# A recurrence beside a projection: plain operand layout, and its steps placed by hand in TensorE's order

## Chip, cores, metric

One NeuronCore of a Trainium2 chip runs the whole program. The metric is the device time of one execution in microseconds (us), as the median of several runs. A profiled execution of the same program is read for the reasons.

## What is computed

One encoder block over 2048 tokens of width 1024. A normed input goes through one projection with 3328 output columns. The first 1792 feed an RWKV-7 mixer with 8 heads of 64, the rest a differential attention with 4 heads. Both results go through an output projection, and a gated convolutional feed-forward layer follows. The change is about the mixer, whose core is this recurrence over the tokens:

```python
def step(S, inp):
    r_t, w_t, k_t, v_t, a_t, b_t = inp
    sa = jnp.einsum('bhvk,bhk->bhv', S, a_t)
    S = (S * w_t[:, :, None, :] + sa[..., None] * b_t[:, :, None, :]
         + v_t[..., None] * k_t[:, :, None, :])
    return S, jnp.einsum('bhvk,bhk->bhv', S, r_t)
```

The mixer around it shifts the projected columns by one token, makes decay, rate and gate from them, normalizes each head's output, adds a bonus term and multiplies by the gate. Everything is held in float32. The large products split each operand into a high and a low part and add three products.

## The kernel before

**Stages.** `phase1` projects four token blocks of 512 tokens. For the mixer's 14 column groups of 128 (`proj_rwkv`, then `shift`) it takes 24 matmuls of 512 columns each, for token blocks 0 to 3. Then come the attention's columns in six groups of 256 (`proj_qk`, `proj_v` by way of `token_major`), 96 matmuls of 256 columns each, for token blocks 3, 0, 1, 2, so 24 groups in all. While token blocks 1 and 2 go through, nine pieces of attention (`head`) are started. After that, attention and feed-forward follow until the end (L968 is a line of the latter).

**The recurrence.** `rwkv(u)` handles a unit of 128 tokens, as two chunks of 64, for all 8 heads (4 pairs `i` times 2 halves `hd`); there are 16 units. A unit loads its columns from DRAM and makes head norms (`st`, then a reciprocal root on VectorE in some dozen small operations, then `nx`, transposed as `nb`), decay (`lpw`) and rate (`lpa`), and products with cumulated decays (`xm`, `bk`). TensorE forms the score products `sa`, and VectorE masks them. A 64-row triangular system has to be inverted per head and chunk. Its 32-row diagonal parts go through DRAM (`ed`) into `el`, are eliminated on VectorE by 31 pairs of dependent operations (`tl`, `wl`, L482 and L483) and return by `wd` into `tt`; `zp` adds the remaining corner. Then the two chunks run one after the other: `gp`, `up`, `hu` and the output `y`, with ScalarE or VectorE between them; the state goes from chunk to chunk. The tail normalizes and gates `y` and writes `yd`.

**Layout.** `xm` and `sh` hold per head a 128-row operand in which one half belongs to the state and the other to the chunk's tokens, and which half is which depends on the chunk and the head. So `gp` is one product of 128 rows, while `y` is a sum of two products for each head, which are issued in turn:

```python
for hd in range(2):
    for i in range(GP):
        nc.tensor.matmul(y4[yq, i, hd, :], xm[c][:, i, hd, C:2 * C], sh[c][:, i, hd, :], start=True, stop=False)
        nc.tensor.matmul(y4[yq, i, hd, :], rb[ub, i, hd, :], su[c][ub, i, hd, :], start=False, stop=True)
```

**Order.** The order of the instructions on every engine is fixed when the program is built, by a scheduler that takes ready work by priority. `unit()` starts one unit behind each two column groups and lets a unit that was started two units earlier go on; both with a priority raised by `HP = 3000`. So the recurrence's products stand wherever the scheduler's own clock saw them ready, in the middle of the projection's.

Of the kernel before, what the change touches and what calls it, by code (L numbers as in the profile page):

```python
# [28 lines left out]
XUB = 7  # L29
SUB, LRB, PUB, UB = 3, 3, 3, 2  # L30
# [9 lines left out]
LAG = 2  # L40
HP, HA1, HA = 3000, 400, 0
# [98 lines left out]
def phase1(g, ctx):  # L140
# [38 lines left out]

    def spread(tb):  # L180

        rs = rsa[:, 4 * tb:4 * tb + 4]
        rx = dn.tile([P, 4, P], F32, name="rx", tag="x", bufs=XB)
        nc.vector.tensor_copy(rx, rs.unsqueeze(2).broadcast_to((P, 4, P)))
        ps = ps_mm.tile([P, 4, P], F32, name="tp", tag="mm")
# [19 lines left out]
    def proj_rwkv(tb, hT, b, w=None, ps=None):  # L205
# [26 lines left out]
    def token_major(tb, hT, gi):  # L232
# [4 lines left out]
        for jj in range(2):  # L237
            for q in range(KT // 2):
                for j2 in range(2):
# [6 lines left out]
                    if q == KT // 2 - 1:  # L246
                        yield 2 * jj + j2, ps

    def proj_qk(tb, hT, gi):
# [12 lines left out]
        return lambda: finish_qk(tb, gi, qz, rs)  # L262

    def finish_qk(tb, gi, qz, rs):
# [3 lines left out]
        for hl_ in range(2):  # L268
# [15 lines left out]

    def proj_v(tb, hT, gi):
# [5 lines left out]

    w = load_w("w_in_a", 12, 4, P, True)
# [3 lines left out]
    stats(0)  # L296
    rb = spread(0)
# [9 lines left out]
    mask = cp.tile([P, P], F32, name="mask")  # L307
    nc.sync.dma_start(out=mask, in_=a["c_mask"])
# [42 lines left out]
    for i in range(UB):  # L351
        tts.append(cp.tile([P, NCH, GP, C], F32, name=f"tt{i}"))
# [5 lines left out]
    hc = cp.tile([P, GP, C], F32, name="hc")  # L358
    nc.vector.memset(hc, 0.0)
    def rwkv(u):  # L360
# [8 lines left out]
        r = sp.tile([P, GP, SB], F32, name="zl", tag="zl", bufs=1)  # L369
# [3 lines left out]
        xm = [sp.tile([P, GP, 2, P], F32, name="xm", tag="xm", bufs=XUB) for c in range(NCH)]  # L373
        bk = [sp.tile([P, GP, P], F32, name="bk", tag="bk", bufs=XUB) for c in range(NCH)]
        rb = sp.tile([P, GP, 2, C], F32, name="rb", tag="rb", bufs=(XUB + 1) // 2)
        lr = sp.tile([P, NCH, GP, C], F32, name="lr", tag="lr", bufs=LRB)
# [8 lines left out]
        nst = 2 * GP  # L385
        nrm = sp.tile([P, nst], F32, name="nrm", tag="nrm")
        rsqrt(g, sp, nrm, st.rearrange("p i h -> p (i h)"), 1.0, L2_EPS, nst, "k")
        nx = sp.tile([P, nst, 64], F32, name="nx", tag="tmp", bufs=2)
        nc.scalar.copy(nx, nrm.unsqueeze(2).broadcast_to((P, nst, 64)))

        lpw = ps_tp.tile([P, GP, SB], F32, name="lpw", tag="tp")
# [9 lines left out]
        for p in range(GP):  # L401
            nc.scalar.activation(kh[:, p], lpa[:, p], AF.Tanh, bias=hw0[:, 4 + p:5 + p], scale=0.5)
        nb = ps_tp.tile([P, GP, SB], F32, name="nb", tag="tp")
# [17 lines left out]
        for c in range(NCH):  # L421
            cs, kc, uc = slice(c * C, c * C + C), slice(c * C, c * C + C), slice(C - c * C, 2 * C - c * C)
            for hd in range(2):
                q = hb[hd]
                nc.vector.tensor_mul(xm[c][q, :, hd, 0:C], kkn[q, :, cs], pp[q, :, c, 0:C])
                if hd == 0:
                    nc.vector.tensor_mul(bk[c][:, :, uc], kkn[:, :, cs], an[:, :, cs])
                nc.vector.tensor_mul(xm[c][q, :, hd, C:2 * C], r[q, :, cs], pp[q, :, c, 1:C + 1])
            nc.vector.tensor_mul(bk[c][:, :, kc], kh[:, :, cs], pin[:, :, cs])
# [4 lines left out]
        nc.gpsimd.tensor_mul(rkh, kh, r)  # L434
        sb = ps_tp.tile([P, GP, 2], F32, name="sb", tag="tp")
# [5 lines left out]
        def mk(q, a, b):  # L441
            return mask[q, a:b].unsqueeze(1).broadcast_to((64, GP, b - a))

        for c in range(NCH):
            for hd, q, q_ in ((0, lo_, hi_), (1, hi_, lo_)):
                sa = ps_sc.tile([P, GP, P], F32, name="sa", tag="sa")
                for i in range(GP):
                    nc.tensor.matmul(sa[:, i, :], bk[c][q, i, :], xm[c][q, i, hd, :], start=True, stop=True)
                kb, ub = hb[c], hb[1 - c]
# [4 lines left out]
        bkt = bk  # L454
        for c in range(NCH):
            ps = ps_sc.tile([P, GP, P], F32, name="bt", tag="sa")
            bs = bk[c]
            for i in range(GP):
                nc.scalar.activation(bs[:, i], bs[:, i], AF.Identity, scale=pc[:, i, c])
                nc.tensor.transpose(ps[:, i, :], bs[:, i, :], ident)  # L460
            nc.scalar.copy(bkt[c], ps)
# [3 lines left out]
        cp3 = lambda t: t.rearrange("s c p t -> s (c p) t")  # L465
        for hd in range(2):
            for hf in range(2):
                r = slice(hd * 64 + hf * 32, hd * 64 + hf * 32 + 32)
                nc.sync.dma_start(out=ed[hd, hf].rearrange("g s t -> s g t"), in_=cp3(lr[r, :, :, hf * 32:hf * 32 + 32]))
# [16 lines left out]
        yield  # L486
        for hd in range(2):
            for hf in range(2):
                r = slice(hd * 64 + hf * 32, hd * 64 + hf * 32 + 32)
                nc.sync.dma_start(out=cp3(tt[r, :, :, hf * 32:hf * 32 + 32]), in_=wd[hd, hf].rearrange("g s t -> s g t"))  # L490
        t11 = sp.tile([P, NCH, GP, 32], F32, name="t11", tag="t11")
        for hd in range(2):
            r1 = slice(hd * 64, hd * 64 + 32)
            nc.vector.transpose(t11[r1].rearrange("s c p t -> s (c p) t"), tt[r1, :, :, 0:32].rearrange("s c p t -> s (c p) t"))
# [4 lines left out]
        nc.sync.dma_start(out=zg, in_=g.zd[tb, 13, :, sl])  # L499
        su = [sp.tile([P, GP, 2, C], F32, name="su", tag="su", bufs=SUB) for c in range(NCH)]  # L500
        sh = [sp.tile([P, GP, 2, C], F32, name="sh", tag="sh", bufs=SUB) for c in range(NCH)]
# [6 lines left out]
        for c in range(NCH):  # L508
            for hd in range(2):
                nc.scalar.copy(sh[c][hb[1 - hd], :, hd], v4[hb[c], :, hd])  # L510
            nc.scalar.copy(su[c][hb[c]], v4[hb[c]])

        zt = sp.tile([P, NCH, GP, 32], F32, name="zt", tag="gt")
# [624 lines left out]
```

## Time and profile before

| | |
|---|---|
| median of 3 runs | 3273.06 us (3269.57 to 3291.25) |
| profiled execution, its own time | 3270.93 us |
| its span, first to last instruction | 3269.2 us |
| TensorE busy | 3136.8 us (96%) |
| VectorE busy | 2085.0 us (64%) |
| ScalarE busy | 1524.9 us (47%) |
| mean granted TensorE clock | 0.972 |

In the profile PE is TensorE (PEld its weight loads), DVE VectorE, ACT ScalarE, POOL GpSimd, SP the queue that issues the DMAs. L569 is line 569 of the kernel. Float32 products appear as two records each, so 16 records stand for 8 products; transposes and the products of the projections have one. A record's duration is not the time that TensorE gives to it, because matmuls overlap; that is read from one start to the next.

### The profile page before, as it was taken

Reading aid. Unit: us, or ns where it says so; the run is one execution under the profiler, and the core shown is the slowest. Engines: PE = TensorE matmul, PEld = TensorE weight load, DVE = VectorE, ACT = ScalarE, POOL = GpSimd, SP = SyncE. Lnnn points to the kernel's source line nnn. Section 1 sums busy time; section 2 is a strip of 40 time slices with the busy share of each in tenths; the row PEclk is TensorE's granted clock in tenths of the full one; section 3 lists DMA queues with packets and bytes.
Section 4 is the critical chain, followed back from the end, with each engine's and each line's share of the span. In section 5 each row is a group of like instructions: output and inputs, shape, how many; then the busy total and the mean of one; then the engine's idle time right before and its main releaser. Section 6 shows DMA issues by size and latency. Waiting matters only on the chain.

```text
span 3269.2 us, 54217 instructions
## 1 busy us (share of the span) xinstructions
PE 3136.8 (96%) x19314; PEld 2657.6 (81%) x19314; DVE 2085.0 (64%) x5939; ACT 1524.9 (47%) x3391; POOL 661.0 (20%) x501
## 2 busy tenths in 40 slices
PE   8999999999999898899999999999998999999999
PEld 6777777888888788788878888888888888888887
DVE  4788778888873565667777786666533444444444
ACT  5666555655645564444445565444423322222221
POOL 4112113342322013254444111111100000000000
PEclk9989999989999899999999999999999999999999
DMA  9765544345464977556556756565574132223222
GB/s 298 252 210 155 189 141 152 105 134 153 126 183 132 290 233 262 160 192 204 197 196 222 234 174 203 168 206 184 192 281 153 65 116 84 97 91 107 87 97 97
DMA packets 395006, 557.43 MB, mean 171 GB/s; under 512 B 82544, under 2 KB 209776, under 8 KB 394608
## 3 DMA queue, kind: packets, MB, share of 16 engines
q1 hardware_dynamic: 394736, 553.97, 52.9%
q8 instruction: 153, 2.51, 0.3%
q14 instruction: 117, 0.96, 0.1%
HBM read 440.59 MB, written 113.25 MB: 169 GB/s over the span
## 4 chain that ended last, share of the span: by engine, by line
PE 80%; DMA 9%; DVE 8%; ACT 1%; issue 1%; SPq 1%; POOL 0%; DVEq 0%; ACTq 0%; POOLq 0%
PE up L968 9%; PE up L966 9%; PE up L967 9%; PE dn L1010 5%; PE dn L1009 5%; PE dn L1011 5%; PE mm L213 3%; PE mm L211 3%; PE mm L212 3%; PE mm L243 2%; PE y L571 2%; PE y L569 2%; PE mm L244 2%; PE mm L245 2%; PE up L906 2%; DMA fwlo<-lo_w_out 2%
## 5 line engine op out<-in xcount | busy, mean ns | idle before, releaser
L967 PE MATMUL up<-hT,fwhi 128*128 128x512 f32 (+1 forms) x1536 | 581.3, 379 | 0.0
L966 PE MATMUL up<-hT,fwhi 128*128 128x512 f32 (+1 forms) x1536 | 575.4, 378 | 3.7 <-DVE halo L975 2.8
L968 PE MATMUL up<-hT,fwlo 128*128 128x512 f32 (+1 forms) x1536 | 571.6, 378 | 7.0 <-DMA fwlo<-lo_w_ffn_up 7.0
L973 DVE SCALAR_TENSOR_TENSOR yy<-up,vec,yy 128x511 f32<-128x511 f32 x352 | 262.0, 744 | 346.2 <-ACT yy L970 345.9
L1012 DVE TENSOR_TENSOR acc<-dn,acc 128x512 f32<-128x512 f32 x352 | 237.0, 688 | 184.0 <-PE dn L1011 183.2
L968 PEld LDWEIGHTS up<-hT,fwlo 128*128 128x128 f32 x1536 | 292.2, 190 | 62.6 <-DMA fwlo<-lo_w_ffn_up 10.4
L966 PEld LDWEIGHTS up<-hT,fwhi 128*128 128x128 f32 x1536 | 290.2, 190 | 57.8 <-issue 4.3
L967 PEld LDWEIGHTS up<-hT,fwhi 128*128 128x128 f32 x1536 | 291.9, 190 | 52.4
L996 POOL TENSOR_TENSOR gl<-yy,gh 128x512 fp32r<-128x512 f32 (+1 forms) x64 | 106.0, 1656 | 1006.4 <-ACT gh L995 821.8
L117 ACT CAST fwhi<-fwraw 128x1024 fp32r<-128x1024 f32 x164 | 172.5, 1052 | 266.1 <-PE up L967 185.5
L970 ACT ACTIVATE yy<-up,vec 128x512 f32<-128x512 f32 x176 | 136.6, 777 | 301.2 <-PE up L968 295.9
L1010 PE MATMUL dn<-dlo,gh 128*128 128x512 f32 x704 | 276.1, 393 | 0.9 <-DMA dlo<-lo_w_ffn_down 0.9
L729 DVE CUSTOM_DVE_ANT_0 e<-sc,nd 128x512 f32<-128x512 f32 (+3 forms) x320 | 188.3, 607 | 136.9 <-PE sc L726 112.9
L1009 PE MATMUL dn<-dhi,gh 128*128 128x512 f32 x704 | 272.5, 396 | 0.5 <-ACT gh L995 0.5
L1011 PE MATMUL dn<-dhi,gl 128*128 128x512 f32 x704 | 261.9, 393 | 0.1
L243 PE MATMUL mm<-whi,hh 128*128 128x256 f32 x768 | 232.7, 304 | 11.9 <-DVE qlo L105 5.4
L244 PE MATMUL mm<-wlo,hh 128*128 128x256 f32 x768 | 227.2, 297 | 7.7 <-DMA wlo<-lo_w_in_b 7.5
L245 PE MATMUL mm<-whi,hl 128*128 128x256 f32 x768 | 225.0, 296 | 0.0
L736 ACT ACTIVATE e<-e,nm 128x1024 f32<-128x1024 f32 (+4 forms) x192 | 171.9, 898 | 53.3 <-DVE nm L733 52.9
L211 PE MATMUL mm<-hh,whi 128*128 128x512 f32 x448 | 187.8, 421 | 9.2 <-ACT hh L201 6.9
L117 ACT CAST whi<-wraw 128x512 fp32r<-128x512 f32 x208 | 127.8, 619 | 138.5 <-PE mm L212 61.8
L213 PE MATMUL mm<-hh,wlo 128*128 128x512 f32 x448 | 187.2, 419 | 2.1 <-POOL wlo L119 2.1
(278 smaller groups left out, 7322.6 us busy)
## 6 DMA issues: line engine op xcount, KB each, us to landing
fwraw<-in_w_ffn_up_dram SPq DMA_DIRECT2D x132, 512.0 KB, 5.5
fwlo<-lo_w_ffn_up SPq DMA_DIRECT2D x88, 512.0 KB, 5.0
draw<-in_w_ffn_down_dram SPq DMA_DIRECT2D x132, 256.0 KB, 4.3
vg<-vd SPq DMA_DIRECT2D x128, 256.0 KB, 4.3
wraw<-in_w_in_a_dram SPq DMA_DIRECT2D x112, 256.0 KB, 3.5
wraw<-in_w_in_b_dram SPq DMA_DIRECT2D x96, 256.0 KB, 5.1
lo_w_ffn_up<-fwlo SPq DMA_DIRECT2D x44, 512.0 KB, 2.9
dlo<-lo_w_ffn_down SPq DMA_DIRECT2D x88, 256.0 KB, 4.9
```

What stands on the lines that cost most here:

```text
L117: nc.scalar.copy(hi, raw)
L211: nc.tensor.matmul(ps, whi[k], hh[k], start=k == 0, stop=False)
L213: nc.tensor.matmul(ps, wlo[k], hh[k], start=False, stop=k == KT - 1)
L243: nc.tensor.matmul(ps, hh[k][:, ts_], whi[k], start=k == 0, stop=False)
L244: nc.tensor.matmul(ps, hh[k][:, ts_], wlo[k], start=False, stop=False)
L245: nc.tensor.matmul(ps, hl[k][:, ts_], whi[k], start=False, stop=k == KT - 1)
L966: nc.tensor.matmul(ps[:, q], wh[:, k % 4, cs], xh, start=k == 0, stop=False)
L967: nc.tensor.matmul(ps[:, q], wh[:, k % 4, cs], xl, start=False, stop=False)
L968: nc.tensor.matmul(ps[:, q], wl[:, k % 4, cs], xh, start=False, stop=k == KT - 1)
L1009: nc.tensor.matmul(ps, gh_[:, tsl], dh_, start=gi == 0, stop=False)
L1010: nc.tensor.matmul(ps, gh_[:, tsl], dl_, start=False, stop=False)
L1011: nc.tensor.matmul(ps, gl_[:, tsl], dh_, start=False, stop=gi == FG - 1)
```

## The change

It rewrites the recurrence's layout and the place of its steps.

- **Layout.** `ar` and `bk` hold per pair and chunk 128 plain rows (both heads), made by four products on VectorE where there were twelve; the masked scores of a chunk and head become one tile `sm`, by one masking where there were three. The state is kept block by block in `hs`. In the chunk loop one product of 128 columns per pair (`ar` by `h`) gives what `gp` and the first half of `y` gave; two further groups of 8 products (with `sm`) add the tokens' parts. The copies into `sh`, and the operand `rb`, are gone.
- **Steps.** `rwkv` yields between its steps: ten up to the inverse, four from its result to `zp`, six for the two chunks, four for the tail. `tick()` runs after every 6 matmuls of a mixer projection and after every 12 of an attention projection, and issues the next steps of up to three units. Inside `manual_schedule` TensorE takes its instructions in the order of the source. The other engines' order is still the scheduler's, now without the raised priority (`HP = 0`). It closes when the last unit has finished.
- **Moved.** `spread` (row norms) goes behind the first projection of a token block, the transposes of `finish_qk` into the next group's pieces, the reciprocal root of the head norms behind `lpa`.

```diff
+XUB, SMB = 3, 6
+UNITS = 3
+HP, HA1, HA = 0, 400, 0
@@ proj_rwkv, in the loop over k
             nc.tensor.matmul(ps, wlo[k], hh[k], start=False, stop=k == KT - 1)
+            if k % 2:
+                tick()
@@ token_major, in the loop over q
+                tick()
+                if 4 * jj + q in (4, 6) and fins:
+                    fins.pop(0)()
@@
+    order = ExitStack()
+    order.enter_context(tc.manual_schedule(engines={mybir.EngineType.PE}))
+    def step(n, to):
+        with tc.high_priority(offset=HP):
+            if stage[n] and next(stage[n][0], "next") == "next":
+                unit = stage[n].pop(0)
+                if to:
+                    stage[to].append(unit)
+    def tick():
+        nonlocal ticks
+        ticks += 1
+        st = stage
+        if not st["chain"] and st["ready"]:
+            st["chain"].append(st["ready"].pop(0))
+        behind = len(st["ahead"]) + len(st["inverse"]) + len(st["ready"])
+        if not st["inverse"] and not st["ready"] and (len(st["ahead"]) > 1 or st["ahead"] and not st["first"] and (not units or behind + len(st["chain"]) == UNITS)):
+            st["inverse"].append(st["ahead"].pop(0))
+        behind = len(st["ahead"]) + len(st["inverse"]) + len(st["ready"]) + len(st["chain"])
+        if not st["first"] and units and (units[0] + 1) * SB <= done * TB and behind < UNITS:
+            st["first"].append(rwkv(units.pop(0)))
+        if ticks % 2:
+            step("chain", "last")
+            if ticks % 8 == 1 or not st["chain"]:
+                step("first", "ahead")
+        else:
+            step("last", None)
+            step("inverse", "ready")
+            step("first", "ahead")
@@ rwkv
+        yield
         lpa = ps_tp.tile([P, GP, SB], F32, name="lpa", tag="tp")
...
+        yield
+        nst = 2 * GP
+        nrm = sp.tile([P, nst], F32, name="nrm", tag="nrm")
+        rsqrt(g, sp, nrm, st.rearrange("p i h -> p (i h)"), 1.0, L2_EPS, nst, "k")
...
+        nc.vector.tensor_mul(ar4[:, :, 1:3], ch(kkn), pp[:, :, :, 0:C])
+        nc.vector.tensor_mul(bk4[:, :, 1:3], ch(kkn), ch(an))
+        nc.vector.tensor_mul(ar4[:, :, 0::3], ch(r), pp[:, :, :, 1:C + 1])
+        nc.vector.tensor_mul(bk4[:, :, 0::3], ch(kh), ch(pin))
...
-                nc.vector.tensor_mul(lr[q, c], sa[ub, :, 0:C], mk(ub, 0, C))
-                nc.vector.tensor_mul(rb[ub, :, hd], sa[ub, :, C:], mk(ub, C, P))
-                nc.vector.tensor_mul(xm[c][q_, :, hd], sa[kb], mk(kb, 0, P))
+                    nc.tensor.matmul(sa[:, i, :], bk[q, i, c], ar[q, i, c], start=True, stop=True)
+                nc.vector.tensor_mul(sm[c][:, :, hd], sa, mk[c])
+            yield
...
+        for c in range(NCH):
+            kb, ub, h, h_ = hb[c], hb[1 - c], hs[c], hs[1 - c]
+            hp = sp.tile([P, GP, C], F32, name="hp", tag="hp")
+            for hd, q in enumerate(hb):
+                nc.gpsimd.tensor_mul(hp[q], h[q, :, hd], pc[q, :, c].broadcast_to((64, GP, C)))
+            gy = ps_y.tile([P, GP, 2, C], F32, name="gy", tag="y")
+            for i in range(GP):
+                nc.tensor.matmul(gy[:, i], ar[:, i, c], h[:, i], start=i == 0, stop=False)
+            for n, (i, hd) in enumerate(ih):
+                nc.tensor.matmul(gy[ub, i, hd], sm[c][kb, i, hd, ub], su[c][kb, i, hd], start=False, stop=n == len(ih) - 1)
+            gt = sp.tile([P, GP, 2, C], F32, name="gt", tag="gt")
+            nc.scalar.copy(gt[ub], gy[ub])
+            yield
+            up = ps_ch.tile([P, GP, 2, C], F32, name="up", tag="ch")
+            for i, hd in ih:
+                nc.tensor.matmul(up[ub, i, hd], tt[ub, i, hd], gt[ub, i, hd], start=True, stop=True)
+            nc.scalar.copy(su[c][ub], up[ub])
+            yield
+            hu = ps_ch.tile([P, GP, C], F32, name="hu", tag="ch")
+            for hd, q in enumerate(hb):
                 for i in range(GP):
+                    nc.tensor.matmul(hu[q, i], bk[:, i, c, q], su[c][:, i, hd], start=True, stop=True)
+            for hd, q in enumerate(hb):
+                nc.vector.tensor_add(h_[q, :, hd], hu[q], hp[q])
+            for n, (i, hd) in enumerate(ih):
+                nc.tensor.matmul(gy[kb, i, hd], sm[c][:, i, hd, kb], su[c][:, i, hd], start=False, stop=n == len(ih) - 1)
+            nc.scalar.copy(yt[kb], gy[kb].rearrange("p i h d -> p (i h d)"))
+            yield "next" if c == NCH - 1 else None
```

## Rows read from the trace of the kernel before

**Rows 1.** Page part 4, chain that ended last, by engine.
```profile
PE 80%; DMA 9%; DVE 8%; ACT 1%; issue 1%; SPq 1%; POOL 0%; DVEq 0%; ACTq 0%; POOLq 0%
```

**Rows 2.** By stretch: length, busy us (instructions) of PE, PEld, DVE, ACT, POOL; clock; DMA share, GB/s.
```profile
100.00:572.00 472.00, 466.89 (x3204) 371.21 (x3204) 387.01 (x1270) 279.97 (x702) 93.42 (x93) 0.93 0.58 179
572.00:1050.00 478.00, 455.41 (x4264) 400.96 (x4263) 364.74 (x1195) 276.51 (x895) 145.80 (x134) 0.94 0.47 139
1050.00:1230.00 180.00, 157.12 (x1124) 145.92 (x1124) 106.29 (x487) 110.97 (x373) 23.44 (x17) 0.92 0.82 252
```

**Rows 3.** Timeline of TensorE, 579 to 606 us: start, us, engine, line.
```profile
580.62 0.97 PE L559 MATMUL hu<-su,bk 128*64 128x64 f32 x16
581.51 0.38 PE L243 MATMUL mm<-whi,hh 128*128 128x256 f32 x1
...
582.06 0.33 PE L569 MATMUL y<-sh,xm 128*64 128x64 f32 x2
582.32 0.32 PE L571 MATMUL y<-su,rb 64*64 64x64 f32 x2
582.58 0.33 PE L569 MATMUL y<-sh,xm 128*64 128x64 f32 x2
...
590.10 1.16 PE L399 MATMUL lpa<-zw,wda 64*128 64x128 f32 x8
591.19 0.38 PE L245 MATMUL mm<-whi,hl 128*128 128x256 f32 x1
```

**Rows 4.** Table by stretch, around two falls of the granted clock.
```profile
579.00:585.80 6.80, 6.80 (x64) 5.52 (x62) 5.62 (x19) 4.88 (x26) 1.53 (x2) 1.00 0.10 39
585.80:589.20 3.40, 3.40 (x27) 3.07 (x27) 3.02 (x11) 1.50 (x4) 0.11 (x1) 0.50 0.12 36
...
633.00:637.00 4.00, 0.00 (x0) 0.00 (x0) 3.73 (x11) 0.00 (x0) 1.49 (x2) 1.00 0.15 58
637.00:640.40 3.40, 3.32 (x15) 3.10 (x15) 3.32 (x9) 1.87 (x5) 1.54 (x2) 0.50 0.55 161
```

**Rows 5.** Groups by line, VectorE, 100 to 1050 us: busy us, mean ns | idle before.
```profile
L452 DVE TENSOR_TENSOR xm<-sa,mask 64x512 f32<-64x512 f32 x64 | 44.1, 689 | 1.0
L428 DVE TENSOR_TENSOR xm<-zl,pp 64x256 f32<-64x256 f32 x64 | 30.3, 473 | 4.1 <-PE y L569 3.9
L425 DVE TENSOR_TENSOR xm<-kkn,pp 64x256 f32<-64x256 f32 x64 | 29.6, 463 | 19.5 <-PE y L569 18.6
L450 DVE TENSOR_TENSOR lr<-sa,mask 64x256 f32<-64x256 f32 x64 | 27.0, 422 | 27.1 <-PE sa L448 25.8
L451 DVE TENSOR_TENSOR rb<-sa,mask 64x256 f32<-64x256 f32 x64 | 26.7, 418 | 0.8
L420 DVE TENSOR_TENSOR an<-an,pin 128x512 f32<-128x512 f32 x16 | 12.4, 778 | 3.9 <-ACT pin L414 2.5 <-ACT an L416 1.4
```

**Rows 6.** DMA issues, 100 to 1050 us: KB each, median us to landing.
```profile
el<-ed SPq DMA_DIRECT2D x128, 64.0 KB, 2.2
...
ed<-lr SPq DMA_DIRECT2D x64, 32.0 KB, 1.6
wd<-wl SPq DMA_DIRECT2D x64, 32.0 KB, 2.0
tt<-wd SPq DMA_DIRECT2D x64, 32.0 KB, 1.9
```

**Rows 7.** Timeline of VectorE: the inverses' first operation; longest; last.
```profile
134.04 0.19 DVE L482 TENSOR_TENSOR tl<-wl,el 128x31 f32<-128x31 f32 x1 [0.36 <-DMA el<-ed]
...
779.33 0.18 DVE L482 TENSOR_TENSOR tl<-wl,el 128x31 f32<-128x31 f32 x1
...
835.16 0.16 DVE L483 TENSOR_TENSOR wl<-wl,tl 128x8 f32<-128x8 f32 x1
...
934.48 1.05 DVE L482 TENSOR_TENSOR tl<-wl,el 128x31 f32<-128x31 f32 x1
...
966.69 0.17 DVE L483 TENSOR_TENSOR wl<-wl,tl 128x8 f32<-128x8 f32 x1
```

More of the change, by code (lines that the diff above doesn't have):

```diff
@@ L267, in finish_qk, with piece @@
         nc.gpsimd.tensor_mul(q3, q3, rs.unsqueeze(2).broadcast_to((P, 16, 64)))
-        for hl_ in range(2):
+        def piece(hl_):
             h = (gi - 7) % 2 * 2 + hl_
@@ L290, in proj_v @@
             nc.sync.dma_start(out=g.vd[t0:t0 + P, :, (gi - 11) * 256:(gi - 10) * 256], in_=vs.bitcast(F32))
+    units = list(range(g.ntb * TB // SB))
+    stage = {n: [] for n in ("first", "ahead", "inverse", "ready", "chain", "last")}
+    done = ticks = 0
+    order = ExitStack()
[26 more added lines that the diff above has]
+            step("first", "ahead")
     w = load_w("w_in_a", 12, 4, P, True)
@@ L522, in rwkv @@
-        for hd in range(2):
-            r1 = slice(hd * 64, hd * 64 + 32)
-            r2 = slice(hd * 64 + 32, hd * 64 + 64)
-            for c in range(NCH):
-                for i in range(GP):
-                    nc.tensor.matmul(zp[r1, 1, c, i, :], zt[r2, c, i, :], tt[r2, c, i, 32:64], start=True, stop=True)
-            nc.scalar.copy(tt[r1, :, :, 32:64], zp[r1, 1])
-        for hd in range(2):
-            q = slice(hd * 64, hd * 64 + 64)
-            nc.vector.tensor_copy(sh[0][q, :, hd, :], hc[q])
@@ L574, in rwkv @@
-        nh, w = 2 * GP, GP * P
+        yield
+        zt = sp.tile([P, GP, 2, 32], F32, name="zt", tag="gt")
+        zp = ps_sc.tile([P, 2, GP, 2, 32], F32, name="zp", tag="sa")
+        ih = [(i, hd) for i in range(GP) for hd in range(2)]
+        for b in range(2):
+            r1 = slice(b * 64, b * 64 + 32)
+            r2 = slice(b * 64 + 32, b * 64 + 64)
+            for i, hd in ih:
+                nc.tensor.matmul(zp[r2, 0, i, hd], sm[1 - b][r1, i, hd, r2], t11[r1, i, hd], start=True, stop=True)
@@ new lines, in rwkv @@
+        for b in range(2):
+            r2 = slice(b * 64 + 32, b * 64 + 64)
+            nc.scalar.copy(zt[r2], zp[r2, 0])
+        yield
+        for b in range(2):
+            r1 = slice(b * 64, b * 64 + 32)
+            r2 = slice(b * 64 + 32, b * 64 + 64)
+            for i, hd in ih:
+                nc.tensor.matmul(zp[r1, 1, i, hd], zt[r2, i, hd], tt[r2, i, hd, 32:64], start=True, stop=True)
+        for b in range(2):
+            r1 = slice(b * 64, b * 64 + 32)
+            nc.scalar.copy(tt[r1, :, :, 32:64], zp[r1, 1])
@@ L593, in rwkv @@
         nc.gpsimd.tensor_add(yt, yt, vt)
+        yield
+        yield
+        yield
+        y = ps_sc.tile([P, w], F32, name="y", tag="sa")
+        nc.tensor.matmul(y, zg, wgu, start=True, stop=True)
         nc.vector.tensor_mul(yt, y, yt)
         nc.sync.dma_start(out=g.yd[u * SB:(u + 1) * SB, :], in_=yt)
-    units = list(range(g.ntb * TB // SB))
-    started = []
-    def unit():
-        if units:
-            with tc.high_priority(offset=HP):
-                started.append(rwkv(units.pop(0)))
-                next(started[-1])
-        if started and (len(started) > LAG or not units):
-            with tc.high_priority(offset=HP):
-                next(started.pop(0), None)
     def head():
@@ L611, in head, with after @@
             next(g.heads, None)
-    def after(done):
-        if (units and (units[0] + 1) * SB <= done * TB) or (started and not units):
-            unit()
-        if not units and not started and g.att is None and 2 in g.phases:
+    def after():
+        if not units and not any(stage.values()) and g.att is None and 2 in g.phases:
+            order.close()
             rctx.close()
@@ L630, in phase1 @@
                     continue
-                shift(tb, b, proj_rwkv(tb, hT, b), rb)
+                ps = proj_rwkv(tb, hT, b)
+                rb = rb or spread(rx)
+                shift(tb, b, ps, rb)
             if gi == 0 and tb + 1 < nb:
-                stats(tb + 1)
-            after(tb)
+                rx = stats(tb + 1)
+        done = tb + 1
     nh = 0
@@ L648, in phase1 @@
                 nh += 1
-    while units or started:
-        after(nb)
+    while units or any(stage.values()):
+        tick()
+    after()
     if 2 not in g.phases:
```

177 lines of the change are left out of this document (59 added, 118 removed).

## The prediction

> **What bounds the kernel now.** The first view is the chain of work that ended last: four fifths of it is TensorE [rows 1]. So I look for the stretch in which the change lies and ask what TensorE does there. The table by stretch gives it: from 100 to 572 us the mixer's projections of token blocks 1 to 3 run with the recurrence between them, from 572 to 1050 the attention's projections with the rest of the recurrence, and by 1230 the projections are over [rows 2]. In the 950 us of the first two, TensorE idles only (472.0 - 466.9) + (478.0 - 455.4) = 27.7 us. VectorE is busy 387 + 365 = 752 us of them, 79%: much, but not the bound. Work on VectorE, ScalarE or the queues is therefore worth only what it makes TensorE wait; TensorE's own time is worth all of it. Yet its busy time hides two losses. The first is in its timeline, read from start to start: 16 records of `hu` take 581.51 - 580.62 = 0.89 us, 0.056 each, while the records of `y`, no wider, take 582.58 - 582.06 = 0.52 us for four, 0.13 each [rows 3]. These alternate between two shapes, 128*64 and 64*64; those of `hu` do not. The second is the granted clock, 0.93 and 0.94 in the two stretches [rows 2]. It has two levels, so it stood at the lower, 1.2 GHz, for 2 x 0.07 x 472 + 2 x 0.06 x 478 = 123 us. If all of that were matmul time, half of it, 62 us, is lost.
>
> **The sum is made against the profiled execution**, 3270.93 us, whose span is 3269.2; it lies 2 us under the median of the runs. After 1230 us nothing is edited, and the chain that ended last is mostly TensorE's work [rows 1], so a gain before it should arrive at the end nearly whole.
>
> **Layout on TensorE.** Per chunk, `gp` (16 records at 0.056, 0.9 us) and `y` (32 records at 0.13, 4.1 us) are 5.0 us. They become 4 products of 128 columns and two groups of 8 small ones, each group of one shape. The 128-column records are priced by `lpa`, 8 records in 591.19 - 590.10 = 1.09 us; each group of 16 records by `hu`, 0.89 us [rows 3]. That is 2.9 us, so 2.1 us less for each of 32 chunks: **-68 us**. `up`, `hu`, `sa` and `zp` keep count and shape. This is the surest term, because TensorE is the bound where it lies. Its low end, if one of the two small groups cost per record what those of `lpa` do (0.136), is 1.3 us less per chunk, -27; for more than 68 there is no row.
>
> **Clock.** At 585.8 the clock fell although TensorE had been busy for all of the 6.8 us before, most of it `y` in turns; at 637 it fell after 4 us of idleness [rows 4]. Both causes exist. The first kind should mostly go, since the alternation is gone and no more than two or three short steps stand between two pieces of projection; the second follows the waits. I take half of the 62 us: **-30**, with ends 0 and -62. The Trainium skill (TensorE: Matmul & The Clock Gate, Part 1, "What's actually happening") makes idleness what returns the clock to its lower level. By that rule alone the change would return nothing here, and the sum would be 30 us higher; the fall at 585.8, behind a fully busy stretch, speaks against taking the rule alone.
>
> **Waits of TensorE in order.** Before, the scheduler put a product where it saw it ready and filled the time with projection. Now a step whose operand is late stops everything behind it: the next piece of projection, and through it the evictions of `shift` and `finish_qk` and the next units' steps. Counting ticks in the diff, the steps run over 280 ticks, from the first projection of token block 1 to the 14th of the 24 attention groups, so a tick lasts some 881 / 280 = 3.1 us. The chunk steps stand two ticks apart, 6 us for one copy or addition: covered. `nb` stands three or four ticks behind `st`, `sa` two or three behind `nb`; with VectorE three quarters busy these are tight. `lpw` and `lpa` follow `st` one tick apart in one PSUM buffer, which VectorE or ScalarE must have read first. `zp` waits for the inverse and is the subject of a rival. No row shows these waits. One end is that all goes well and the old idleness vanishes too, -28; the other is the rival's. I take **+25**, about as much again as the 27.7 us that the scheduler's own fixed order left [rows 2], since it too is an order that cannot be changed when something is late.
>
> **Other engines.** Masking takes 4 x (422 + 418 + 689) = 6.1 us per unit and becomes four operations priced like the longest, 2.8 us; `xm` takes 4 x (473 + 463) = 3.7 us and becomes two of 128 x 512 at 778 ns, 1.6 us [rows 5]. So VectorE loses 5.5 us per unit, 88 us in all, the `bk` products, the state copies and ScalarE's copies into `sh` apart. That is counted at nothing, because TensorE's work covers it; if VectorE were the bound it would be worth up to 88. It shortens the waits above. The unit's DMAs (three loads, `ed`, `el`, `wd`, `tt`, two loads, one store) stay the same in number on SP's queue but lose their raised priority, and `hp` on POOL is of the same size; both are hidden by several ticks. Hand-overs between projection and recurrence cost a little at each place; there were as many before, so nothing. `spread` behind the first projection removes a short wait per token block, included in the old idleness.
>
> **Tail.** The last unit ends in the 14th attention group instead of the 16th, and the pieces of attention start one group later. From 1050 to 1230, without recurrence to fill in, TensorE idles 22.9 us over a third of the groups, DMA being busy 0.82 of the time [rows 2]. That is almost 3 us per group, so **+4** for one and a half more groups; ends 0 and 15.
>
> Sum: -68 - 30 + 25 + 4 = -69, so **3202 us**.
>
> **Rivals.**
>
> *B, everything falls into place.* No waits and a full clock: -68 - 62 - 28 + 4 = -154, 3117 us. For it: the steps are spaced with some slack, and VectorE has less to do. Against it: the tight places named above.
>
> *C, slower: the inverse comes later than its step.* The step that stores `ed` and the first `zp` stand 17 ticks apart for every second unit and 26 for the others, 53 and 81 us. The way between takes 1.6 + 2.2 + 2.0 + 1.9 = 7.7 us of DMA [rows 6] and the inverse, 62 operations in a row on VectorE: 56.0 us for the longest, 32.4 for the last, when VectorE has little else [rows 7]. In the middle (44) it needs 52 us and is just covered; at 56 it needs 64, and TensorE stands still for 11 us in eight units, 88 us, and loses some 14 more to the clock behind each idleness [rows 4]. That is -69 + 88 + 14 = +33, 3304 us. It is slower than before from an inverse of about 52 us on. For it: the raised priority is gone. Against it: VectorE's share falls from 79% to (752 - 88) / 881 = 75%, and while TensorE stands still little new work reaches VectorE. The Trainium skill (SBUF — State Buffer, "Who interferes with whom") lets GpSimd and a VectorE operation with both inputs in SBUF lock each other out; by that rule the inverse stays long whatever TensorE does, as its operations are of this kind and GpSimd's work does not shrink. That is this rival, at its price.
>
> *D, no change: the inverses set the pace.* `el` and `tl` have one buffer, so inverses run one after another; from the first operation at 134.0 to the last at 966.9 there are 833 us for 16, 52 us per unit [rows 7]. If that pace is VectorE's own and not TensorE's, the stretch keeps its length and what TensorE saves turns into waiting: 3265 to 3275 us. Against it: that is some four times 62 operations at the 0.16 to 0.19 us that the first and last of them show, so most of an inverse's time is other work pushed between.
>
> **Chances and range.** The forecast 0.53, B 0.16, D 0.14, C 0.17. A difference under 1%, 33 us, is about what cannot be told from no change here. Under 3238 us lie B and nearly all of the forecast: faster 0.66. D, and the edges of the forecast and of C, are the same: 0.19. Slower 0.15. The range goes from B's 3117, with a little for the layout's far end, to C: 3110 to 3300.
>
> **What would show it.** After: the records of the two new groups with `sm` stand about 0.06 us apart, and `gy` on the whole takes some 3 us per chunk; the granted clock between 100 and 1000 us is 0.96 or more; TensorE's idleness there is between 40 and 70 us, spread over `nb`, `sa` and `zp`; the last `yd` is issued near 970 us; the stretch after the projections keeps its length. The prediction is wrong if waits of `zp` for VectorE's or the DMA's `tt` stand out (C), if the inverses lie end to end while TensorE idles (D), or if the clock stays at 0.93 though nothing waits.

## The result and the profile after

The changed kernel takes 3310.34 us (median of 4 runs, 3303.41 to 3322.34) against 3277.88 for the kernel before (4 runs). The ratio is 1.0111, 95% interval 1.0077 to 1.0145: slower by 1.1%, where 3202 us was forecast. Its profiled execution has a span of 3301.6 us, 32.4 more than before. The chain of work that ended last still is mostly TensorE's, but less so than in [rows 1], and DMA and VectorE have more of it:

```profile
PE 69%; DMA 13%; DVE 10%; ACT 3%; issue 2%; SPq 2%; POOL 1%; DVEq 0%; ACTq 0%; POOLq 0%
```

The table by stretch, with the columns and the bounds of [rows 2]:

```profile
100.00:572.00 472.00, 432.71 (x3165) 347.04 (x3166) 336.77 (x1134) 269.77 (x649) 100.83 (x100) 0.91 0.54 163
572.00:1050.00 478.00, 425.43 (x3939) 385.26 (x3938) 321.33 (x1071) 267.45 (x819) 143.77 (x129) 0.92 0.51 148
1050.00:1230.00 180.00, 147.62 (x1068) 138.51 (x1068) 98.07 (x436) 111.59 (x404) 19.98 (x14) 0.91 0.77 239
```

Read the first two numbers of a row (its length, and what TensorE is busy of it) against each other: TensorE idles 39.3 + 52.6 = 91.9 us in the first two stretches, where it idled 27.7 before. The clock is 0.91 and 0.92 instead of 0.93 and 0.94, although VectorE has 94 us less to do. What TensorE waits for there (instruction, what it waited for: us in total, times, longest):

```profile
PE lpw L440 <- DVE rq_x_k L87: 15.6, 4, 10.9
PE sb L491 <- POOL rkh L486: 13.3, 5, 5.3
PE nb L459 <- ACT kh L450: 8.0, 7, 2.4
```

`zp`, the step of rival C, is not among the first twelve of that list. The longest wait shows how such a thing comes about. The timeline of the kernel after (start, us, engine, line; in brackets the idle time before and what ended it):

```profile
890.92 1.64 SPq L517 DMA_DIRECT2D ed<-sm  x2
...
896.30 0.18 DVE L87 TENSOR_SCALAR rq_x_q<-qss 128x16 f32<-128x16 f32 x1 [2.63 <-ACT qsq L264]
898.82 0.80 SPq L523 DMA_DIRECT2D el<-ed  x2
899.00 0.28 PE L247 MATMUL mm<-whi,hl 128*128 128x256 f32 x1
901.27 3.57 SPq L523 DMA_DIRECT2D el<-ed  x5
908.90 0.19 DVE L530 TENSOR_TENSOR tl<-wl,el 128x31 f32<-128x31 f32 x1 [12.43 <-DMA el<-ed]
909.93 0.16 DVE L87 TENSOR_SCALAR rq_x_k<-st 128x8 f32<-128x8 f32 x1
910.15 2.07 PE L440 MATMUL lpw<-zw,wda 64*128 64x128 f32 x8 [10.87 <-DVE rq_x_k L87]
```

`lpw` is written to the one PSUM buffer that `st` was written to (PSUM is where this kernel puts its products). It comes free when the first operation of the reciprocal root has read `st` (`rq_x_k`). That operation is ready, but it stands in VectorE's queue behind the first operation of the other unit's inverse (`tl`), and this waits 12.43 us for `el`. So a late transfer stops VectorE, and through it TensorE, with all the projection that is queued behind `lpw`. The table around it shows what the clock makes of it:

```profile
893.00:899.30 6.30, 6.28 (x53) 6.03 (x51) 0.84 (x2) 4.88 (x22) 3.05 (x4) 1.00 0.47 156
899.30:904.30 5.00, 0.00 (x0) 0.00 (x0) 0.00 (x0) 0.00 (x0) 0.75 (x1) 1.00 0.49 125
904.30:910.10 5.80, 0.00 (x0) 0.00 (x0) 1.20 (x13) 0.00 (x0) 0.00 (x0) 0.50 0.39 101
910.10:914.50 4.40, 4.35 (x19) 4.13 (x20) 4.40 (x29) 1.62 (x5) 1.90 (x1) 0.50 0.44 145
```

TensorE, VectorE and ScalarE stand still together from 899.3 on, GpSimd nearly so; the clock falls to 1.2 GHz within the wait and stays there for 4.4 us of the work behind it. VectorE's own waits for these transfers, first after, then before, 100 to 1050 us:

```profile
DVE tl L530 <- DMA el<-ed: 41.7, 12, 12.4
DVE t L542 <- DMA tt<-wd: 39.0, 22, 5.9
```

```profile
DVE t L494 <- DMA tt<-wd: 5.4, 4, 2.9
DVE tl L482 <- DMA el<-ed: 4.6, 3, 2.1
```

The time that the masks and products on VectorE no longer take comes back as waiting for DMA: 10 us before, 81 after. The layout itself does what it should. Per chunk, TensorE's timeline of the kernel after, start to start:

```profile
599.68 1.10 PE L609 MATMUL gy<-su,sm 128*64 128x64 f32 x16
600.71 0.50 PE L211 MATMUL mm<-hh,whi 128*128 128x512 f32 x1
...
700.99 1.05 PE L591 MATMUL gy<-hs,ar 128*128 128x128 f32 x8
701.97 1.14 PE L593 MATMUL gy<-su,sm 64*64 64x64 f32 x16
703.05 0.66 PE L280 MATMUL tp<-ident,qz 128*128 128x128 f32 x4
```

That is 0.98 + 1.08 + 1.03 = 3.1 us per chunk where `gp` and `y` took 5.0.

### The profile page after: what moved, and what is told of

It reads as the page before. It is cut to its first block, busy times and chain, and to the rows that moved or that the text cites. A ratio compares the mean times of both kernels' runs of the same rounds, so it can differ in the third digit from the quotient of the medians.

```text
span 3301.6 us, 53239 instructions
## 1 busy us (share of the span) xinstructions
PE 3090.5 (94%) x19058; PEld 2637.9 (80%) x19058; DVE 1977.0 (60%) x5668; ACT 1515.8 (46%) x3311; POOL 667.4 (20%) x501
## 4 chain that ended last, share of the span: by engine, by line
PE 69%; DMA 13%; DVE 10%; ACT 3%; issue 2%; SPq 2%; POOL 1%; DVEq 0%; ACTq 0%; POOLq 0%
PE up L996 9%; PE up L994 9%; PE up L995 9%; PE dn L1038 5%; PE dn L1039 5%; PE dn L1037 5%; PE mm L211 2%; PE mm L212 2%; PE mm L213 2%; DMA fwlo<-lo_w_out 2%; PE up L934 2%; PE sc L753 2%; PE mm L245 2%; DVE tl L530 1%; DVE wl L531 1%
## 5 line engine op out<-in xcount | busy, mean ns | idle before, releaser
L995 PEld LDWEIGHTS up<-hT,fwhi 128*128 128x128 f32 x1536 | 290.9, 189 | 52.6 <-DVE hT L105 0.3
L211 PE MATMUL mm<-hh,whi 128*128 128x512 f32 x448 | 199.6, 445 | 15.5 <-ACT hh L201 15.1
L212 PE MATMUL mm<-hl,whi 128*128 128x512 f32 x448 | 185.2, 413 | 6.5 <-DVE hl L202 6.5
```

The lines of the kernel that those rows point to most:

```text
L995: nc.tensor.matmul(ps[:, q], wh[:, k % 4, cs], xl, start=False, stop=False)
```

## Experiments

All times are medians; ratios are to the kernel before, run on the same chip.

**First: one part alone, or one undone.** In the kernel before, only `y`'s products are grouped by shape (b_y_grouped):

```diff
+            ih = [(i, hd) for hd in range(2) for i in range(GP)]
+            for n, (i, hd) in enumerate(ih):
+                nc.tensor.matmul(y4[yq, i, hd, :], xm[c][:, i, hd, C:2 * C], sh[c][:, i, hd, :],
+                                 start=n == 0, stop=False)
+            for n, (i, hd) in enumerate(ih):
+                nc.tensor.matmul(y4[yq, i, hd, :], rb[ub, i, hd, :], su[c][ub, i, hd, :],
+                                 start=False, stop=n == len(ih) - 1)
```

> The kernel before with only the output products reordered: per chunk the 8 products with xm first, then the 8 with rb, in place of taking turns. Theory that the layout's gain is real (a record of y costs 0.13 us in turns and 0.056 in a group): y falls from 4.1 to 1.8 us per chunk, 2.3 x 32 = 74 us, so 3190 to 3215 us, and no full-clock stretch ends behind a block of y any more. Rival, that the alternation costs nothing because the time is set by VectorE or by the inverses: 3260 to 3280 us.

3276.92 us, ratio 1.0003 [0.9976, 1.0030]: no change. In the trace the saving is there, since the last output of the recurrence starts at 994 us instead of 1053; but the last attention projection ends at 1229 us, as it did before. So it is not true that what TensorE saves ahead of 1050 us arrives at the end. TensorE idles 70.7 us up to there, where it idled 27.7:

```profile
100.00:1050.00 950.00, 879.32 (x7477) 757.78 (x7477) 763.37 (x2546) 555.64 (x1606) 242.35 (x229) 0.91 0.55 164
```

In the changed kernel the order by hand is taken away (a_free_order); layout and steps stay:

```diff
-    order.enter_context(tc.manual_schedule(engines={mybir.EngineType.PE}))
```

> The changed kernel with TensorE's order left to the scheduler again (layout, steps and their places in the source stay). Theory that the order in the source causes the waits: TensorE's idleness between 100 and 1050 us falls from 93 us to 30 or 40, the clock rises from 0.91 to 0.94 or more, and the time to 3200 to 3250 us. Rival, that operands are simply late because the steps are short and unprioritized: idleness stays above 70 us and the time within 3290 to 3320.

3272.98 us, 0.9993 [0.9968, 1.0017]: the order by hand costs 37 us of 3310. Its row of the table by stretch: TensorE idles 43.3 us there, 49 less than with the order by hand, but the clock is as low.

```profile
100.00:1050.00 950.00, 906.74 (x7230) 783.11 (x7229) 669.16 (x2218) 547.48 (x1528) 243.10 (x229) 0.91 0.53 159
```

The priority is given back with the order by hand kept (a_raised_priority, `HP = 3000`), and the reciprocal root is moved right behind `st`, so that `lpw`'s buffer comes free earlier (a_root_behind_st):

```diff
         for p in range(GP):
             nc.tensor.matmul(st[:, p, :], sq[:, p], ones2, start=True, stop=True)
+        rsqrt(g, sp, nrm, st.rearrange("p i h -> p (i h)"), 1.0, L2_EPS, nst, "k")
+        nx = sp.tile([P, nst, 64], F32, name="nx", tag="tmp", bufs=2)
+        nc.scalar.copy(nx, nrm.unsqueeze(2).broadcast_to((P, nst, 64)))
...
-        rsqrt(g, sp, nrm, st.rearrange("p i h -> p (i h)"), 1.0, L2_EPS, nst, "k")
```

> The changed kernel with the steps' priority raised by 3000 again, TensorE's order still that of the source. Theory that the lost priority makes VectorE, GpSimd and ScalarE late for the steps: the waits of lpw, nb and sb (15.6, 8.0 and 16.5 us) fall by more than half, and the time to 3250 to 3285 us. Rival, that lateness comes from the places of the steps in the source: waits stay within a few us, or move to the projection's own operands (hh, qz, vs), and the time stays at 3295 to 3325.

> The changed kernel with the reciprocal root of the head norms issued right behind its sums, as in the kernel before, in place of behind lpa. lpw waits 15.6 us for the first operation of that root, which has to read the one buffer that lpw writes next. Theory that it is this place alone: those 15.6 us and the slow clock behind them go, 3285 to 3295 us. Rival, that one wait gone only shows the next (nb, sb): 3300 to 3320 us.

With the priority (a_raised_priority) 3314.44 us, 1.0111 [1.0067, 1.0155]; with the root moved (a_root_behind_st) 3308.61 us, 1.0075 [1.0035, 1.0116]. With TensorE in order the priority changes nothing. Moving the root in the source does not cure `lpw`, whose waits sum to 14.2 us, the longest 8.3: the root still stands behind the first operation of an inverse on VectorE, which waits 9.87 us for `el`.

**Second: is it the DMA behind the recurrence that takes the gain?** The low part of the attention's weights is computed and not loaded, in four kernels:

```diff
-    if not first:
+    if not first and kept is not None:
         nc.sync.dma_start(out=lo.bitcast(F32), in_=kept)
     nc.scalar.copy(hi, raw)
-    if first:
+    if first or kept is None:
         nc.gpsimd.tensor_sub(lo, raw, hi.bitcast(F32))
+    if first and kept is not None:
         nc.sync.dma_start(out=kept, in_=lo.bitcast(F32))
@@ load_w, the argument kept
-kept[:, k0:k0 + n]
+None if name == "w_in_b" else kept[:, k0:k0 + n]
```

> The kernel before, with one edit: the low part of the attention's weights (w_in_b) is no longer stored to DRAM and loaded again, but made anew by a subtraction on GpSimd (128 x 512, 1.35 us each, four per attention group). That takes 1 MB from each group's traffic, some 4 us at the 250 GB/s that this stretch moves. Theory: once the recurrence is over, the attention's groups are paced by the DMA (busy 0.84 there, 21.6 us per group), so about 8 groups shorten by 2 to 4 us each: 3240 to 3257. Rival: something else paces those groups, and the time stays within 8 us of the kernel before.

> The kernel before with both edits: y's products grouped by shape, and the low part of the attention's weights made on GpSimd. Theory: the 60 us by which the grouping ends the recurrence earlier were given back because 10.8 groups instead of 8.2 then run at the DMA's pace; with less traffic a part of them arrives, so this kernel lies 15 to 40 us below the one with the second edit alone: 3205 to 3235. Rival: the gain is given back whatever the DMA does, and this kernel stands within 8 us of that one.

> The changed kernel, with the low part of the attention's weights made on GpSimd. Theory: its 10 groups behind the recurrence shorten by 2 to 4 us each, and the waits in order stay: 3270 to 3290. Rival, if these groups are not paced by the DMA: 3305 to 3315.

> The changed kernel without the order by hand for TensorE, and with the low part of the attention's weights made on GpSimd: the new layout, the scheduler's order, the lighter traffic. Theory: no change before (3273) because of the DMA's pace, so now 15 to 45 us below the kernel before with the lighter traffic alone: 3200 to 3235. Rival: level with that one within 8 us.

b_lo_computed takes 3324.94 us, 1.0146 [1.0098, 1.0194]; b_y_lo_computed 3268.17, 0.9972 [0.9949, 0.9996]; a_lo_computed 3292.32, 1.0056 [1.0037, 1.0076]; a_free_lo_computed 3255.81, 0.9940 [0.9915, 0.9965]. The theory is mostly wrong. Behind the recurrence an attention group became 0.7 to 1.6 us shorter (216 us for 10.0 groups after, 200 for the same groups with the edit), not 2 to 4. And the kernel before, which has less to move, became 49 us slower. It also gives GpSimd the subtractions, and its recurrence ends 39 us later; how much of the 49 is theirs and how much another order, this run does not separate.

**Third: the chain through VectorE.** The elimination is cut (`for s in range(8)` in place of 31), which leaves out 23 of its 31 pairs of operations and with them the right result, so that only the time is read; and in one kernel the steps stand wider apart instead:

> The kernel before, with the elimination cut from 31 pairs of VectorE operations per unit to 8 (23 pairs left out). It takes away what the recurrence waits for between its scores and its corner product. Theory: before, TensorE is the bound (idle 28 us of the 953 in which the recurrence runs), so little is to be gained: 3240 to 3270. Rival: the chain through VectorE already sets the pace here: under 3220.

> The changed kernel without the order by hand, with the elimination cut from 31 pairs to 8. Theory: the layout gives TensorE some 55 us less to do, and the chain of each unit through VectorE keeps the stretch from shrinking by as much, so that TensorE waits and its clock falls. With that chain cut the saving arrives: 3195 to 3230, at least 25 us below the kernel before with the same cut. Rival: what takes the saving is not this chain (the clock, or the scheduler's fixed order), and the two stand within 12 us of each other.

> The changed kernel with its order by hand and the elimination cut from 31 pairs to 8. Theory: the steps that stop TensorE (lpw for the first operation of the reciprocal root, nb, sb) are late because what they need stands in VectorE's queue among the operations of an inverse, so the waits between 100 and 1040 us fall from 86 to 40 to 60 and the time by 25 to 50: 3260 to 3285. Rival: they are late by GpSimd's, ScalarE's and the loads' own delays, and the time stays within 12 us of the changed kernel, 3298 to 3322.

```diff
+        yield
         yield
         lpw = ps_tp.tile([P, GP, SB], F32, name="lpw", tag="tp")
...
+        yield
         yield
         yield
         sb = ps_tp.tile([P, GP, 2], F32, name="sb", tag="tp")
```

> The changed kernel with one more empty step between st and lpw and one more ahead of sb, so 12 steps instead of 10 up to the inverse. Theory: the waits at these two places (some 29 of 86 us) mostly go, and as the steps up to the inverse set the pace of the units the recurrence ends one to two attention groups later, with fewer groups behind it: 3280 to 3300. Rival: TensorE waits for the same things at the next steps, so that nothing is won: 3305 to 3325.

b_short_inverse takes 3299.51 us, 1.0049 [1.0018, 1.0081]; a_free_short_inverse 3265.87, 0.9970 [0.9951, 0.9990]; a_short_inverse 3256.88, 0.9941 [0.9918, 0.9963]; a_wider_steps 3281.93, 1.0015 [0.9992, 1.0039]. With TensorE in order, the cut is worth 53 us, a little over the expected 25 to 50, but not for the expected reason: `lpw`'s longest wait is still 10.8 us and `sb`'s waits sum to 16.5. Of the 45 us between the two profiled executions 21 are won by the last attention projection (it ends at 1235 us against 1256); the other 24 lie behind it, where nothing was edited. The wider steps win 28 us, the expected size. `lpw`'s wait is gone and `sb`'s fell, but `zp` now waits, as in rival C, so that TensorE's idleness up to 1050 us falls only from 91.9 to 86.6 (TensorE's waits of this kernel, 100 to 1050 us):

```profile
PE zp L569 <- DVE t L544: 14.9, 2, 8.7
...
PE sb L493 <- POOL rkh L487: 7.3, 2, 4.5
```

The kernel before, with a quarter of the inverse's operations, is slower by a half per cent. That was expected by neither theory, and with the 49 us above it raised the question of the order itself.

**Fourth: queue, priority, and both cures together.** `ed` and `el` issued by `nc.gpsimd.dma_start`; `HP = 0` in the kernel before; the changed kernel without the order by hand with `HP = 3000`; wider steps with the computed low part.

> The changed kernel with the transfers ed and el issued from GpSimd's queue and not from SP's. Theory: el is late because its issues stand in SP's queue among the weights' and the projections' stores, and VectorE waits for it with the reciprocal root behind; so tl's waits for el fall from 41.7 to under 20 us, lpw's wait of 10.9 us goes, and the time falls by 10 to 25: 3285 to 3300. Rival: the round trip itself (store, then load) is what VectorE waits for, and GpSimd, which now stands behind it, makes rkh and hp late: 3305 to 3330.

> The kernel before with the raised priority of the recurrence set to 0, as in the change, and nothing else. Theory: the order of the kernel before is better than its neighbours (two kernels that only leave work out of it were 24 and 49 us slower), so this edit, which changes no work, costs too: 3285 to 3330. Rival: the priority does nothing, 3268 to 3284.

> The changed kernel without the order by hand and with the raised priority of the kernel before: the layout and the division into steps, in the scheduler's order. Theory: the priority has no direction of its own, so the time stays near the one without it, 3260 to 3290. Rival: the lost priority hid the layout's gain, and with it the time is 3200 to 3245.

> The changed kernel with the two empty steps more, and with the low part of the attention's weights made on GpSimd. Theory: the two edits won 28 and 18 us at different places (waits in order, traffic behind the recurrence), so they add: 3255 to 3272, below both kernels. Rival: both won time in the same stretch, and together they give no more than the better one: 3275 to 3290.

a_ed_el_on_pool_queue takes 3340.71 us, 1.0188 [1.0151, 1.0224]; b_no_priority 3324.59, 1.0149 [1.0103, 1.0195]; a_free_raised 3282.27, 1.0020 [0.9999, 1.0041]; a_wider_lo_computed 3298.73, 1.0064 [1.0038, 1.0089]. On the other queue the waits that the theory named do go, `tl`'s for `el` from 41.7 to 7.9 us and `lpw`'s from 15.6 to 0.6, and the kernel is 30 us slower all the same: now `tt` stands out among VectorE's waits, and TensorE waits for it and for GpSimd (waits of VectorE, then of TensorE, in this kernel, 100 to 1050 us):

```profile
DVE t L542 <- DMA tt<-wd: 61.6, 22, 6.1
```

```profile
PE sb L491 <- POOL rkh L486: 16.1, 4, 4.8
PE zp L567 <- DVE t L542: 15.1, 4, 6.2
PE nb L459 <- ACT kh L450: 12.6, 8, 4.1
```

The two cures do not add; together they are 17 us worse than the wider steps alone. And taking the priority from the kernel before, which the prediction counted at nothing, costs 48 us by itself.

**Fifth: does the saving arrive without the priority?** `y` grouped with `HP = 0`, and the kernel before with `HP = 1000`:

> The kernel before with y's products grouped by shape and the recurrence's priority 0. Theory: at priority 0 TensorE's saving of some 60 us arrives, as it did for the new layout, so this kernel lies 35 to 65 us below the kernel before at priority 0: 3260 to 3290. Rival: there the new layout gained by its shorter work on VectorE or its steps and not by TensorE's products, and this kernel stays at 3305 to 3335.

> The kernel before with the recurrence's priority at 1000 instead of 3000. Theory: the kernel before stands on a favourable order and any other one costs, so 3290 to 3330. Rival: what costs is the recurrence coming last among the ready work, and a smaller lead is as good as the larger, 3268 to 3284.

b_y_no_priority takes 3237.87 us, 0.9885 [0.9859, 0.9910], and b_priority_1000 3272.54, 0.9987 [0.9964, 1.0010]. The first is the fastest kernel of all, below both, with an edit of a few lines: at priority 0 the grouping is worth 87 us, at 3000 nothing. The row of this kernel and, below it, that of the kernel before with priority 0 (100 to 1050 us):

```profile
100.00:1050.00 950.00, 889.46 (x7657) 771.83 (x7656) 757.09 (x2544) 567.82 (x1653) 244.26 (x230) 0.92 0.56 169
```

```profile
100.00:1050.00 950.00, 918.22 (x7277) 768.75 (x7277) 736.98 (x2450) 543.70 (x1545) 234.53 (x224) 0.91 0.51 155
```

TensorE is busy for 29 us less and has done 380 records more. `HP = 1000` gives the same instructions in the same order on every engine as `HP = 3000`, so that run leaves its question open. It serves as a repeat instead: what two traces of one program differ by.

**All of them beside each other**, from 100 us to the end of each profiled execution. "Own work" sums every TensorE record's distance to the next start, but at most the median for its line; "idle" is time with no record running; "lower clock" is the time at 1.2 GHz, idle or not. The us are medians; the other columns are of the one profiled execution, which in a_wider_lo_computed is its slowest, 20 us above the median.

| kernel | us | own work | idle | lower clock |
|---|---|---|---|---|
| before | 3276 | 2823 | 114 | 187 |
| same order again (b_priority_1000) | 3273 | 2822 | 117 | 202 |
| b_short_inverse | 3300 | 2822 | 135 | 231 |
| b_no_priority | 3325 | 2834 | 140 | 267 |
| b_lo_computed | 3325 | 2822 | 138 | 266 |
| b_y_grouped | 3277 | 2761 | 160 | 257 |
| b_y_lo_computed | 3268 | 2762 | 160 | 226 |
| b_y_no_priority | 3238 | 2758 | 138 | 210 |
| a_free_order | 3273 | 2760 | 133 | 263 |
| a_free_raised | 3282 | 2759 | 149 | 225 |
| a_free_lo_computed | 3256 | 2756 | 135 | 187 |
| a_free_short_inverse | 3266 | 2761 | 135 | 227 |
| after | 3310 | 2765 | 194 | 242 |
| a_raised_priority | 3314 | 2767 | 203 | 243 |
| a_root_behind_st | 3309 | 2766 | 196 | 240 |
| a_lo_computed | 3292 | 2766 | 194 | 210 |
| a_wider_lo_computed | 3299 | 2769 | 195 | 283 |
| a_wider_steps | 3282 | 2768 | 181 | 232 |
| a_short_inverse | 3257 | 2767 | 164 | 215 |
| a_ed_el_on_pool_queue | 3341 | 2766 | 216 | 289 |

Each grouping of shapes, old layout or new, takes some 60 us from TensorE's own work. The scheduler's orders of the old products idle 114 to 140 us, those of the new ones 133 to 160, the orders by hand 164 to 216. Among the kernels with the old products taken in turns, the two in the order of the kernel before are the fastest, and leaving out work (b_short_inverse), or moving it (b_lo_computed), does not help: it brings another order. The three other orders have 21 to 26 us more idleness and 44 to 80 more at the lower clock than the kernel before. The repeat differs by 3 us of idleness and 15 of lower clock, so most of these distances are the orders' own. The granted clocks of all executions bear this out. The time at the lower clock, 2 x (1 - clock) x span, has a median of 203 us in 102 executions of the kernel before (163 to 277), of 276 in b_no_priority (265 to 301) and of 265 in b_y_grouped (229 to 269).

## Why the prediction was wrong

**The balance by its own terms**, from the rows: layout (3.1 - 5.0) x 32 = -61 us (forecast -68); clock +12 (-30): at 0.91 and 0.92 the lower level lasts 2 x 0.09 x 472 + 2 x 0.08 x 478 = 161 us instead of 123 (159 by the trace), but TensorE idles in 18 us of it, and in 5 before, which the next term counts; of the rest, 142 against 118, half of the difference is lost; waits between 100 and 1050 us 91.9 - 27.7 = +64 (+25); tail +13 (+4), where idleness between the recurrence's end and the last projection is 36 us against 23. The sum is +28. The last attention projection ends 27 us later (1256 against 1229), and the other 5 of the spans' 32.4 lie behind it, where nothing is edited. The profiled execution is the fastest of the changed kernel's four, at a mean clock of 0.963 where the others have 0.958 to 0.960, so in the median run the clock takes more.

**The steps that failed are "Waits of TensorE in order", by 39 us, and "Clock", by 42 and in sign.** In the first I drew the cost of an order that nothing can change from the scheduler's idleness. It is larger because the other engines' queues are fixed too, and by another plan: a product that has its operands stops because an operation two places away on VectorE waits for a DMA. Undoing the order by hand alone takes 37 us back, 49 of the idleness with it. For the second, I let half of the lower clock go with the alternation. The falls behind fully busy stretches did go: all 21 falls between 100 and 1050 us have at least 1.1 us of idleness in the 10 us ahead of them, where 12 of 23 had none before. But the falls that are left last longer, 7.6 us on the mean against 5.3. Nor was the alternation the whole cause: the new layout, which has none, shows 10 of 25 falls without idleness when the scheduler orders it (a_free_order), behind stretches with several other groups of small products, and b_y_grouped still 2 of 18. The Trainium skill (TensorE: Matmul & The Clock Gate, Part 1, "What's actually happening") has idleness return the lower clock. The fall at 904.3, within a wait of 10.87 us, agrees; the 12 falls before and the 10 of a_free_order do not. By that rule alone the clock term would have been no gain.

**"A gain before it should arrive at the end nearly whole" failed as well**, and this is the lesson of the first run: the grouping alone moved the recurrence's end by 60 us and the program's by nothing. In the kernel before TensorE was busy for 97% of the stretch from 100 to 1050 us, yet with 60 us taken from its work the idleness rose by 46 us and the time at the lower clock by 70, as the table says.

**The priority was counted at nothing, "hidden by several ticks".** On the kernel before it is worth 48 us. So the change can be walked in three measured steps, priority away +48, layout and steps -52, order by hand +37. But the steps do not commute: with the priority kept, layout and steps are +6 (a_free_raised, within the noise).

**Right were** the size of the layout's term, that recurrence and projections keep their places (it ends with the 14th group), that `nb` is tight, and that VectorE is not the bound. The last `yd`, expected near 970 us, is issued at 1045. Rival C's place was wrong for this kernel: `zp` hardly waits, and the inverses became shorter (24 to 49 us, where they took 32 to 56). Its mechanism, a late DMA result that stops TensorE in order, was the right one at other steps. Rival D, that TensorE's saving turns into waiting, describes the grouping at priority 3000, but the inverses' pace is not shown to be the reason: cutting them left the new layout in the scheduler's order, at priority 0, within 7 us, and the grouping at 3000 was not run with the cut. (The pace of 52 us per unit, which D calls some four times 62 operations of 0.16 to 0.19 us, is nearer five times.) The Trainium skill (SBUF — State Buffer, "Who interferes with whom") has a lock between GpSimd and VectorE, which I set behind rival C; by it the inverses were to stay long. They did not, with GpSimd busy for 245 us of the two stretches against 239, and how much of what is left is that lock, no run separates.

**Open:** why the order of the kernel before has so little lower clock, and why the same saving is worth 87 us in one order and nothing in another. The runs show that it is the order, not which property of it; and as orders of the same work lie up to 48 us apart, one pair of kernels does not tell what a part is worth in general. Nor is it shown why the stretch behind the last projection, which no edit touches, lasts between 2022 and 2080 us. Idleness and clock go with it: in the shortest (a_short_inverse) TensorE idles 57 us and spends 31 at the lower clock, in the longest (a_wider_lo_computed) 80 and 82.

## What to carry to other kernels

When every engine's order is fixed at build time, a part's cost is not a property of the part: measure a control that only reorders (here the priority, +48 us) before you believe a saving or its absence, and try a saving under several priorities. An order by hand for one engine needs slack against the queues of all others: look for the operation that stands ahead, on the engine that frees your buffer, and for what that one waits for, and expect the wait to move when you cure it. And keep the small edit as a candidate: grouping `y`'s products by shape, with the priority dropped, beat both kernels by 1.2 and 2.2%.

## What the runs showed of the hardware

A store to DRAM and the load of the same data behind it took 18 us once: the last two `ed` issues start at 890.92, SP then waits 5.2 us for them to land before `el` goes out, and the inverse begins at 908.90, with the DMA less than half busy (0.39 to 0.49). The medians of the two transfers, 1.6 and 2.2 us [rows 6], had promised a fifth of that. From the waits of SP's queue in the kernel after, 880 to 912 us:

```profile
SPq L523 <- DMA ed<-sm: 5.2, 1, 5.2
```

Small float32 products take half the busy time when those of one shape stand together: nothing but the order of `y`'s products (and with it the place of their `start` flags) is edited between the next two rows, of the groups by line (busy us, mean ns | idle before) of the kernel before and of b_y_grouped, and 85.0 us become 43.0. The other kind goes from 84.2 to 42.1.

```profile
L569 PE MATMUL y<-sh,xm 128*64 128x64 f32 x512 | 85.0, 249 | 5.0 <-DVE yt L594 5.0
```

```profile
L569 PE MATMUL y<-sh,xm 128*64 128x64 f32 x512 | 43.0, 236 | 2.6 <-DVE sh L563 1.8 <-DVE yt L595 0.8
```
